# Where the gate products of the attention stand on TensorE, and where their bias rows come in

## The chip, the core and the metric

The kernel runs on one core of a Trainium2 chip, as one launch. The metric is the device time of that launch in microseconds; the time given for a kernel is the median of its runs. The engines are called PE (TensorE, products; PEld are its weight loads), DVE (VectorE), ACT (ScalarE), POOL (GpSimd) and SP (SyncE, which here only issues loads). Each engine works through its own queue in order. A load can be issued from the queues of SP, ACT and POOL.

## The reference, cut to what matters

One layer of an encoder trunk on 256 tokens of width 2048: windowed attention with 32 query heads and 8 key/value heads, and a squared-ReLU MLP of width 8192. Each of the two is preceded by a scale and shift and followed by a gated residual and a layer norm. Scale, shift and gate are one product of a single vector with a 2048 x 12288 matrix:

```python
c_act = jax.nn.silu(c)
mod = c_act @ mod_w[i] + mod_b[i]
sh_m, sc_m, g_m, sh_f, sc_f, g_f = jnp.split(mod, 6, axis=-1)
hmix = x * (1.0 + sc_m[:, None, :]) + sh_m[:, None, :]
y = windowed_gqa_sink(hmix, ...)             # ... @ w_o + b_o
x = layer_norm(DEEPNORM_ALPHA * x + (1.0 + g_m[:, None, :]) * y, ...)
hff = x * (1.0 + sc_f[:, None, :]) + sh_f[:, None, :]
y = sq_relu_mlp(hff, ...)                    # relu(hff @ w1 + b1) ** 2 @ w2 + b2
x = layer_norm(DEEPNORM_ALPHA * x + (1.0 + g_f[:, None, :]) * y, ...)
```

All numbers are float32. The change touches the two gates `g_m` and `g_f` and the output bias `b_o` of the attention.

## The kernel before

**Weights.** Every weight matrix is cut into blocks of 128 x 2048 floats, 1 MB each, which SP loads in one planned order into "raw" buffers (`Stream.loads`, the DMA of line 209): five buffers of the pool `raws`, and three more of `raws2` up to the middle of the attention. ACT casts each half of a block to a high part (`wh`, line 254) and DVE subtracts to get a low part (`wl`, line 225); five halves of each can be ahead of use. A product of activations with weights is then three matmuls, high by high, high by low and low by high: `mm3`, lines 501 to 503. PE does this work through the whole kernel.

**Modulation.** Between the weight blocks of that planned order stand the blocks of the modulation matrix. They need no split: `Mod.step` multiplies a block with the activated vector `cact`. For most blocks this is done on PE, as a quad of four small matmuls into one PSUM tile `pm`, one for each group of 32 columns of the array (`quad`, line 313). For the blocks listed in `dve` it is done on DVE, which keeps sums per partition in `part`: the first block by a multiply (line 351), the later ones by a multiply-add (line 353); at the end a matmul with a matrix of ones adds the partitions up. A modulation block is called a chunk here.

- `m_gm` is the gate of the attention, 16 chunks, loaded from `in_modgm`. Chunks 5, 9, 12 and 14 go to DVE, the others to PE. At its end a quad with `onesf` adds the sums of DVE, and a quad with `ones` adds the bias, which POOL loads into four small buffers `br` (line 336; tag "t2", four buffers) six chunks before the end.
- `m_gf` is the gate of the MLP, 16 chunks from `in_modgf`, all on DVE, in two `g4b` buffers, during MLP block 1. Its `step` passes through the same line 336 at chunk 10, and so loads four `br` tiles which nothing reads afterwards. At chunk 15, POOL loads the bias in four rows (line 331) and adds them to partition 0 of the sums (line 332).
- `m_mix` and `m_ff` are scale and shift of the two halves, from `in_modm` and `in_modf`; their biases are added elsewhere.

`gate` turns the finished sums into 128 equal rows by a product with ones (line 400). It is called for `m_gm` in step 12 of the attention and for `m_gf` in MLP block 2.

**The attention.** The loop `for n in range(21)` writes scores, softmax, transposes and values (`scores`, `normalise`, `probs_T`, `values`) of step n, and between them weight products: the last four blocks of the query/key/value product for n = 0 to 3, and from n = 5 on one column block of the output product, `project(j, c)`, with j = (n - 5) // 4. The outputs of j = 0 are added to the output bias `bo` (line 852), which `bias_all` spreads over all partitions by two loads from POOL's queue (line 178, 512 KB each) into two of the 20 buffers of the tag `g4`, at n = 0.

**Order.** The program is traced in the order of the code, and a planner then gives each engine its order: of the instructions that its own estimate of durations takes to be ready, the one traced first. So an instruction traced late may stand early on its engine. `Stream.pump` traces chunks ahead of the weight blocks that follow them, whenever a product is half or wholly done (`S.done`). `S.pin` holds the order of some instructions to that of the code, in the first stretch only. A tile takes the place of one that was released, and waits for that release.

**Buffers of the tag `g4b`.** The first call of `g4b` ends the pool `raws2` and puts six buffers of 128 x 1024 floats (`gen2`) in its place. Before the change the first call is at n = 5: four buffers for `ys`, the sums of the output product; at n = 12 two for the gate. After the attention they serve the sums of the MLP, its bias, and the sums and the gate of `m_gf`.

**MLP block 1.** `ff_hidden(1)` computes the hidden columns, four column groups of output products follow (`ff_out`), each evicted by line 1086. With each group, POOL loads two rows `gb` of the layer norm (line 1081, tag "t2" like `br`), and DVE applies them to the residual (lines 1090 and 1091).

Of the kernel before, what the change touches and what calls it, by code (L numbers as in the profile page):

```python
# [11 lines left out]
F32 = mybir.dt.float32  # L12
# [8 lines left out]
S = 256  # L21
# [19 lines left out]
NHIGH = 5  # L41
NLOW = 5
VECS = 2


@with_exitstack
def hybrid_kernel(ctx: ExitStack, tc: tile.TileContext, a, out: bass.AP):
# [17 lines left out]
    def g4b(dt=F32):  # L65
        if not more:
            early.close()
            more.append(ctx.enter_context(tc.tile_pool(name="gen2", bufs=2 * MORE)))
        return more[0].tile([128, 1024], dt, tag="g4b", name="g4b")
# [15 lines left out]
    make_identity(nc, ident)  # L85
    identr = cst.tile([128, 128], F32R, name="identr")
    nc.vector.tensor_copy(identr, ident)
    ones = cst.tile([1, 32], F32, name="ones")
    nc.vector.memset(ones, 1.0)
    onesr = cst.tile([128, 128], F32R, name="onesr")  # L90
    onesf = cst.tile([128, 128], F32, name="onesf")
    nc.vector.memset(onesf, 1.0)
# [81 lines left out]
    def bias_all(src, g4=g4):  # L174

        b = [g4(), g4()]
        for h in range(2):
            nc.gpsimd.dma_start(b[h], src[:, h * 1024:h * 1024 + 1024].partition_broadcast(128))
        return lambda c: b[c // 2][:, (c % 2) * 512:(c % 2) * 512 + 512]


    class Stream:
# [4 lines left out]
        def __init__(self):  # L187
            self.q, self.raw = [], []
            self.hs, self.ls, self.src = [], [], []
            self.free, self.home, self.used = [raws] * RAWS + [raws2] * MORE, [], 0  # L190
            self.of = []
            self.deep = True
            self.at = self.im = 0
            self.nh, self.nl = NHIGH, NLOW
            self.stop = 0
            self.pace = VECS
            self.pin = False
            self.side = {}

        def plan(self, src, use=None, kept=False):  # L200
# [91 lines left out]
    class Mod:  # L292
        def __init__(self, srcs, width, dve=(), bias=None):
            self.srcs, self.dve, self.bias = srcs, set(dve), bias
            self.pairs = width == 64
            self.w = 128 if self.pairs else width
            self.kc = 2048 // (4 * width)
            self.n = NK // self.kc
            self.i = self.planned = 0
            self.whole = len(self.dve) == NK  # L300
            self.first = True
            self.part = None

        def plan(self, n=1):
            for _ in range(n):
# [4 lines left out]
        def quad(self, lhsT, rhs, stop):  # L310
            w = self.w
            for j in range(4):
                i = nc.tensor.matmul(self.ps[32 * j:32 * j + 32, :w], lhsT[j] if type(lhsT) is list else lhsT,  # L313
                                     rhs[j], start=self.first, stop=stop)
                if j == 0:
                    S.pinned(i)
            self.first = False

        def step(self, raw):
            w, kc, i = self.w, self.kc, self.i  # L320
            if i == 0:
                self.ps = psm.tile([128, 512], F32, name="pm")
            r = raw.rearrange("p (k j n) -> p k j n", k=kc // 2 if self.pairs else kc, j=4)
            self.i += 1
            last = self.i == self.n
            per = 1024 // w
            if last and self.whole:
                for n in range(4):
                    b, p = sml.tile([128, 512], F32, name="mrow", bufs=2), self.part[n // 2]
                    p = p[0:1, n % 2 * 512:n % 2 * 512 + 512]  # L330
                    nc.gpsimd.dma_start(b[0:1], self.bias[:, n * 512:n * 512 + 512])
                    nc.gpsimd.tensor_add(p, p, b[0:1])
            elif i == self.n - 6 and self.bias is not None:
                self.br = [sml.tile([128, 512], F32, name="br", tag="t2", bufs=4) for _ in range(4)]
                for n, b in enumerate(self.br):
                    nc.gpsimd.dma_start(b[0:1], self.bias[:, n * 512:(n + 1) * 512])
            for k in range(kc):
                kt = i * kc + k
                if self.pairs:
                    if k % 2 == 0:  # L340
                        cols = [cact[:, kt + j // 2:kt + j // 2 + 1].to_broadcast([128, 32]) for j in range(4)]
                        self.quad(cols, [r[:, k // 2, j] for j in range(4)], last and k == kc - 2)
                elif i in self.dve:
                    e = min(4 * w, 1024)
                    new = self.part is None
                    if new:
                        self.part = [(g4b if self.whole else g4)() for _ in range(4 * w // e)]
                    for n, p in enumerate(self.part):
                        s = raw[:, k * 4 * w + n * e:k * 4 * w + n * e + e]
                        if new:  # L350
                            nc.vector.tensor_scalar(p[:, :e], s, cact[:, kt:kt + 1], None, op0=OP.mult)
                        else:
                            nc.vector.scalar_tensor_tensor(p[:, :e], s, cact[:, kt:kt + 1], p[:, :e],  # L353
                                                           op0=OP.mult, op1=OP.add)
                else:
                    stop = last and k == kc - 1 and not self.dve and self.bias is None
                    self.quad(cact[:, kt:kt + 1].to_broadcast([128, 32]), [r[:, k, j] for j in range(4)], stop)
            if last and not self.whole:
                if self.dve:
                    self.quad(onesf[:, :32], [self.part[j // per][:, (j % per) * w:(j % per) * w + w]  # L360
                                              for j in range(4)], self.bias is None)
                if self.bias is not None:
                    self.quad(ones, [b[0:1] for b in self.br], True)
                self.r = sml.tile([128, 512], F32, name="mrow", bufs=2)
                nc.scalar.copy(self.r[:, :w], self.ps[:, :w])

# [133 lines left out]
    def mm3(ps, xh, xl, wh, wl, start, stop):  # L500
        nc.tensor.matmul(ps, xh, wh, start=start, stop=False)  # L501
        nc.tensor.matmul(ps, xh, wl, start=False, stop=False)  # L502
        nc.tensor.matmul(ps, xl, wh, start=False, stop=stop)  # L503

    XK = [(0, 2), (2, 2), (4, 4), (8, 4), (12, 4)]

# [375 lines left out]
        return out  # L882

    todo = []
    for n in range(21):
        j, i = n // 4, n % 4
        if n < 16:
# [1 line left out]
        for f in todo:  # L889
            f()  # L890
        todo = []
        if n == 0:
            bo = bias_all(a["bo"])
        if n == 1:
            S.deep = False
        if n == 5:
# [1 line left out]
        if n + 2 < len(LATE):  # L898
            w = qkv(*LATE[n + 2])
        elif n < 5:  # L900
            w = iter((0, 1))
        else:
            if n == 5:
                ys = [g4b() for _ in range(4)]
            w = project((n - 5) // 4, (n - 5) % 4)
        S.vecs(SLOT_FILL.get(n, 0) if len(LATE) - 2 <= n < 5 else 0)
        mid = mids(n)
# [24 lines left out]
    def ff_columns(g):  # L932
# [4 lines left out]
        nc.vector.tensor_mul(b2[:, s], lnT[:, 1, s], scf[:, s])  # L937
        nc.vector.tensor_add(b2[:, s], b2[:, s], shf[:, s])

    ff_columns(0)  # L940
    S.stop = 0
    S.vecs(4)
# [272 lines left out]
```

## Time and profile before

| | us |
|---|---|
| median of 3 runs | 1149.16 |
| lowest and highest run | 1144.77, 1152.79 |
| the profiled execution | 1148.29 |
| its span, first to last instruction | 1146.5 |

Mean granted clock of TensorE in the profiled execution: 0.984 of full speed.

In the profile a row of the page's second part has one digit for each fortieth of the span, the busy share in tenths. In lists of instructions, "out<-in" are the program's tile names, and an idle time in brackets is that of the engine just before the instruction, with the instruction or load that ended it. A quad shows as eight matmuls, since a float32 matmul is two instructions. "L313" is line 313 of the kernel. Busy times of PE are modelled and overlap by some tenths of a microsecond.

The loads by source, with the median time from issue to landing in the profiled execution: blocks of `in_modgm` 6.2 us, of `in_modgf` 6.7, of `in_modf` 6.3, the two loads of the output bias 4.8, the `gb` rows 6.2.

### The profile page before, as it was taken

To read this page: it belongs to the slowest core of one execution; us is meant where nothing else is said; L and a number is where in the kernel's file an instruction comes from. 1 tells how busy PE (TensorE), PEld (TensorE's weight loads), DVE (VectorE), ACT (ScalarE), POOL (GpSimd) and SP (SyncE) were. 2 spreads that over 40 slices of the span, in tenths; PEclk is the share of its full clock that TensorE was granted. 3 is DMA by queue.
4 is the path that set the end of the run, shared out by engine and by line. 5 is a ranking of instruction groups with operands and counts; after the bars stand their busy time and mean duration, and the time that the engine had idled before them with its cause. 6 is when DMAs were issued, how large, how long until landed. Compare 5 with 4: busy or idle time off the path is not lost.

```text
span 1146.5 us, 15812 instructions
## 1 busy us (share of the span) xinstructions
PE 1096.7 (96%) x6258; PEld 882.3 (77%) x6258; DVE 810.3 (71%) x1122; ACT 546.9 (48%) x852; POOL 31.8 (3%) x52
## 2 busy tenths in 40 slices
PE   8889999699999999999999998998999999999994
PEld 6667666356776699988888886887888888888883
DVE  5697885757989978765578887756665656665656
ACT  5333554657775455653345542335444334444331
POOL 2000000000000000000000001300000000000001
PEclk9999999979999999999999998999999999999997
DMA  9999997626896798555677788764555555557511
GB/s 377 424 425 425 428 382 245 232 86 218 319 336 224 278 376 330 187 188 204 226 260 280 270 289 298 257 247 157 184 184 190 205 192 184 184 187 258 207 46 73
DMA packets 42946, 288.51 MB, mean 252 GB/s; under 512 B 5100, under 2 KB 5740, under 8 KB 9080
## 3 DMA queue, kind: packets, MB, share of 16 engines
q1 hardware_dynamic: 39824, 279.85, 65.3%
q0 software_dynamic: 2176, 6.32, 1.7%
q10 hardware_dynamic: 872, 1.34, 0.4%
q8 instruction: 49, 0.80, 0.3%
q14 instruction: 25, 0.20, 0.0%
HBM read 285.39 MB, written 2.10 MB: 251 GB/s over the span
## 4 chain that ended last, share of the span: by engine, by line
PE 80%; DMA 9%; DVE 6%; issue 2%; ACT 2%; POOL 0%; DVEq 0%; SPq 0%; ACTq 0%; POOLq 0%
PE pa L501 14%; PE pa L503 14%; PE pa L502 14%; PE pa L1045 13%; PE pa L1046 7%; PE pm L313 4%; DMA raw<-in_modm 3%; PE pa L1022 3%; PE pa L1021 3%; PE pa L1023 3%; DMA raw<-in_modgf 2%; DVE wl L225 2%; PE pa L792 1%; DMA raw<-in_wqkv 1%; PE pt L777 1%
## 5 line engine op out<-in xcount | busy, mean ns | idle before, releaser
L225 DVE TENSOR_TENSOR wl<-raw,wh 128x1024 fp32r<-128x1024 f32 x332 | 405.8, 1228 | 234.5 <-ACT wh L254 233.7
L254 ACT CAST wh<-raw 128x1024 fp32r<-128x1024 f32 x332 | 347.6, 1053 | 457.2 <-PE pa L503 241.5
L501 PE MATMUL pa<-wh,g 128*128 128x512 f32 x816 | 322.4, 396 | 11.3 <-DVE g4b L1086 5.2
L503 PE MATMUL pa<-wh,g 128*128 128x512 f32 x816 | 319.1, 393 | 1.3 <-DVE g L539 1.3
L502 PE MATMUL pa<-wl,g 128*128 128x512 f32 x816 | 319.7, 392 | 0.0
L1045 PE MATMUL pa<-g,wh 128*128 128x512 f32 x768 | 270.3, 397 | 2.9 <-DVE rl L994 2.9
L1046 PE MATMUL pa<-g,wl 128*128 128x256 f32 x768 | 215.5, 281 | 0.0
L501 PEld LDWEIGHTS pa<-wh,g 128*128 128x128 f32 x816 | 153.8, 189 | 52.3 <-DVE g4b L1086 5.9
L503 PEld LDWEIGHTS pa<-wh,g 128*128 128x128 f32 x816 | 153.6, 188 | 38.4 <-DVE g L539 3.4
L502 PEld LDWEIGHTS pa<-wl,g 128*128 128x128 f32 x816 | 154.0, 189 | 31.2 <-issue 1.0
L1045 PEld LDWEIGHTS pa<-g,wh 128*128 128x128 f32 x768 | 144.1, 188 | 38.2 <-DVE rl L994 3.6
L1046 PEld LDWEIGHTS pa<-g,wl 128*128 128x128 f32 x768 | 145.1, 189 | 0.2
L1022 PE MATMUL pa<-g,wh 128*128 128x256 f32 x256 | 72.7, 285 | 0.4 <-DVE g L965 0.4
L1021 PE MATMUL pa<-g,wh 128*128 128x256 f32 x256 | 72.5, 286 | 0.0
L1023 PE MATMUL pa<-g,wl 128*128 128x256 f32 x256 | 72.3, 283 | 0.0
L313 PE MATMUL pm<-raw,cact 128*32 128x256 f32 (+2 forms) x832 | 58.5, 381 | 14.2 <-DMA raw<-in_modgm 9.7
L353 DVE SCALAR_TENSOR_TENSOR g<-raw,cact,g 128x1024 f32<-128x1024 f32 x51 | 65.1, 1278 | 3.7 <-DMA raw<-in_modgm 3.2
L313 PEld LDWEIGHTS pm<-raw,cact 128*32 128x32 f32 x832 | 22.1, 109 | 36.2 <-DMA raw<-in_modgm 10.9
L1021 PEld LDWEIGHTS pa<-g,wh 128*128 128x128 f32 x256 | 48.8, 192 | 1.3 <-issue 0.8
L1022 PEld LDWEIGHTS pa<-g,wh 128*128 128x128 f32 x256 | 49.1, 192 | 0.9 <-DVE g L965 0.8
L1023 PEld LDWEIGHTS pa<-g,wl 128*128 128x128 f32 x256 | 49.1, 192 | 0.0
L353 DVE SCALAR_TENSOR_TENSOR g4b<-raw,cact,g4b 128x1024 f32<-128x1024 f32 x30 | 38.1, 1279 | 9.2 <-DMA raw<-in_modgf 6.8
(180 smaller groups left out, 854.2 us busy)
## 6 DMA issues: line engine op xcount, KB each, us to landing
raw<-in_w SPq DMA_DIRECT2D x64, 1024.0 KB, 4.9
raw<-in_w1b SPq DMA_DIRECT2D x48, 1024.0 KB, 5.0
raw<-in_modm SPq DMA_DIRECT2D x32, 1024.0 KB, 15.8
raw<-in_modf SPq DMA_DIRECT2D x32, 1024.0 KB, 6.3
raw<-in_wqkv SPq DMA_DIRECT2D x24, 1024.0 KB, 14.4
raw<-in_modgm SPq DMA_DIRECT2D x16, 1024.0 KB, 6.2
raw<-in_wo SPq DMA_DIRECT2D x16, 1024.0 KB, 6.5
raw<-in_w1a SPq DMA_DIRECT2D x16, 1024.0 KB, 6.8
```

The source lines that it names most:

```text
L225: self.pinned(nc.vector.tensor_sub(l, r, f32(self.hs[n])))
L254: self.pinned(nc.scalar.copy(h, s))
L313: i = nc.tensor.matmul(self.ps[32 * j:32 * j + 32, :w], lhsT[j] if type(lhsT) is list else lhsT, rhs[j], start=self.first, stop=stop)
L353: nc.vector.scalar_tensor_tensor(p[:, :e], s, cact[:, kt:kt + 1], p[:, :e], op0=OP.mult, op1=OP.add)
L501: nc.tensor.matmul(ps, xh, wh, start=start, stop=False)
L502: nc.tensor.matmul(ps, xh, wl, start=False, stop=False)
L503: nc.tensor.matmul(ps, xl, wh, start=False, stop=stop)
L1021: nc.tensor.matmul(o, wh(w, 128), hh, start=new, stop=False)
L1022: nc.tensor.matmul(o, wh(w, 128), hl, start=False, stop=False)
L1023: nc.tensor.matmul(o, wl(w, 128), hh, start=False, stop=end)
L1045: nc.tensor.matmul(ps, wh(k, 128), hb, start=k == 0, stop=False)
L1046: nc.tensor.matmul(ps[:, :256], wl(k, 128), hb[:, :256], start=False, stop=k == NK - 1)
```

## The change

1. In the attention loop (`S.behind`, set before the loop and cleared behind it), the first matmul of each quad gets an edge of order, without a wait, to the last matmul of the last `mm3` traced above it (`S.prev`). The planner may then not put the quad ahead of that matmul on PE.
2. The sums that DVE keeps for the two gates begin with the bias row. At chunk 4 of `m_gm` and chunk 0 of `m_gf` (`start`), POOL sets the two tiles of `part` to zero and two loads from ACT's queue put the bias into their partition 0. The first DVE chunk is then a multiply-add like the others. The `br` loads, the quad with `ones`, and POOL's loads and additions at the end of `m_gf` are gone.
3. `bias_all(a["bo"])` moves from n = 0 to n = 5 and takes its two buffers from `g4b`.

```diff
+ORDER_ONLY = mybir.DependencyInfo(mybir.DependencyClass.NoSync, mybir.DependencyReason.DATA)
...
-    ones = cst.tile([1, 32], F32, name="ones")
-    nc.vector.memset(ones, 1.0)
...
-            self.pin = False
+            self.pin = self.behind = False
+            self.prev = None
...
+            self.start = -1 if bias is None else max(min(dve) - 1, 0)
...
                 if j == 0:
                     S.pinned(i)
+                    if S.behind and S.prev is not None:
+                        tc.add_manual_dep(i.ins, S.prev.name, ORDER_ONLY, reason="behind")
...
-            if last and self.whole:
-                for n in range(4):
-                    b, p = sml.tile([128, 512], F32, name="mrow", bufs=2), self.part[n // 2]
-                    p = p[0:1, n % 2 * 512:n % 2 * 512 + 512]
-                    nc.gpsimd.dma_start(b[0:1], self.bias[:, n * 512:n * 512 + 512])
-                    nc.gpsimd.tensor_add(p, p, b[0:1])
-            elif i == self.n - 6 and self.bias is not None:
-                self.br = [sml.tile([128, 512], F32, name="br", tag="t2", bufs=4) for _ in range(4)]
-                for n, b in enumerate(self.br):
-                    nc.gpsimd.dma_start(b[0:1], self.bias[:, n * 512:(n + 1) * 512])
+            if i == self.start:
+
+                self.part = [(g4b if self.whole else g4)() for _ in range(2)]
+                for n, p in enumerate(self.part):
+                    nc.gpsimd.memset(p, 0.0)
+                    nc.scalar.dma_start(p[0:1], self.bias[:, n * 1024:n * 1024 + 1024])
...
-                    stop = last and k == kc - 1 and not self.dve and self.bias is None
+                    stop = last and k == kc - 1 and not self.dve
...
-                                              for j in range(4)], self.bias is None)
-                if self.bias is not None:
-                    self.quad(ones, [b[0:1] for b in self.br], True)
+                                              for j in range(4)], True)
...
-        nc.tensor.matmul(ps, xl, wh, start=False, stop=stop)
+        S.prev = nc.tensor.matmul(ps, xl, wh, start=False, stop=stop).ins
...
     todo = []
+    S.behind = True
     for n in range(21):
...
-        if n == 0:
-            bo = bias_all(a["bo"])
...
             if n == 5:
-                ys = [g4b() for _ in range(4)]
+                ys, bo = [g4b() for _ in range(4)], bias_all(a["bo"], g4b)
...
+    S.behind = False
     ff_columns(0)
```

More of the change, by code (lines that the diff above doesn't have):

```diff
@@ L346, in step @@
                     if new:
-                        self.part = [(g4b if self.whole else g4)() for _ in range(4 * w // e)]
+                        self.part = [g4() for _ in range(4 * w // e)]
                     for n, p in enumerate(self.part):
```

## The prediction

> **What bounds the kernel now.** I read the page first, then the list of who waited for whom on PE, then PE's idle stretches by windows, and last the timelines of the engines around them. The page:
>
> ```profile
> PE 1096.7 (96%) x6258; PEld 882.3 (77%) x6258; DVE 810.3 (71%) x1122; ACT 546.9 (48%) x852; POOL 31.8 (3%) x52
> ...
> PE   8889999699999999999999998998999999999994
> ...
> PEclk9999999979999999999999998999999999999997
> ```
>
> TensorE is the bound: it is busy 96% of the span, and each slice is 28.7 us. Behind the start its row dips in slice 7 (201 to 229 us, in the attention), 24 (688 to 717 us) and 27, and the granted clock dips in slices 8 and 24. So the room is in single stalls. The longest waits of PE over the whole run (total us, times, longest us):
>
> ```profile
> PE pm L313 <- DMA raw<-in_modgm: 9.7, 2, 9.0
> PE pa L501 <- DVE g4b L1086: 5.2, 1, 5.2
> ...
> PE pa L1045 <- DVE rl L994: 2.9, 2, 2.6
> ```
>
> The first is a gate chunk of the attention (a step of `m_gm`) that waits for its load, the second a weight product of MLP block 1 that waits for an eviction. What each costs, by windows (us; busy PE, PEld, DVE, ACT, POOL; granted clock; DMA share; GB/s):
>
> ```profile
> 221.30:230.30 9.00, 0.00 (x0) 0.00 (x0) 5.68 (x7) 1.70 (x4) 0.00 (x0) 0.70 0.70 274
> 230.30:236.00 5.70, 5.69 (x20) 1.05 (x21) 0.04 (x1) 1.07 (x2) 0.00 (x0) 0.50 0.84 282
> 236.00:243.00 7.00, 7.00 (x39) 5.05 (x39) 1.46 (x4) 2.75 (x5) 0.00 (x0) 0.57 0.18 73
> 243.00:255.00 12.00, 12.00 (x58) 7.87 (x58) 9.35 (x21) 9.50 (x30) 0.00 (x0) 1.00 0.00 1
> 698.50:703.80 5.30, 0.06 (x2) 0.01 (x1) 5.30 (x8) 0.00 (x0) 0.54 (x1) 0.91 0.95 322
> 703.80:709.70 5.90, 5.90 (x14) 4.64 (x15) 5.90 (x7) 1.04 (x1) 0.54 (x1) 0.51 0.96 310
> 776.30:779.10 2.80, 0.19 (x3) 0.02 (x1) 1.60 (x3) 1.42 (x2) 0.00 (x0) 1.00 0.78 234
> 779.10:785.00 5.90, 5.90 (x33) 5.16 (x34) 5.33 (x10) 3.58 (x7) 0.00 (x0) 1.00 0.16 67
> ```
>
> A long stall is paid twice: behind the 9.0 us one the clock is 0.50 for 5.7 us and 0.57 for 7.0 us, which loses 5.7 x 0.50 + 7.0 x 0.43 = 5.9 us; behind the 5.3 us one it is 0.51 for 5.9 us, 2.9 us lost. The 2.6 us wait at 776 is followed by full clock. So the first stall is worth at most 9.0 + 5.9 = 14.9 us and the second 5.2 + 2.9 = 8.1 us.
>
> [...]
>
> **The change, part by part. (A) The order of gate chunks.** PE in order of time (start, us, what, count, idle before and its releaser):
>
> ```profile
> 206.46 0.39 PE L503 MATMUL pa<-wh,g 128*128 128x512 f32 x1
> 206.78 1.06 PE L313 MATMUL pm<-raw,cact 128*32 128x512 f32 x8
> ...
> 218.09 1.06 PE L313 MATMUL pm<-raw,cact 128*32 128x512 f32 x6 [0.73 <-DMA raw<-in_modgm]
> ...
> 230.31 1.93 PE L313 MATMUL pm<-raw,cact 128*32 128x512 f32 x8 [9.01 <-DMA raw<-in_modgm]
> 232.01 1.93 PE L313 MATMUL pm<-g,onesf 128*32 128x512 f32 x8
> 233.88 1.91 PE L313 MATMUL pm<-br,ones 1*32 1x512 f32 x2
> 235.72 1.25 PE L706 MATMUL pt<-identr,g 128*128 128x128 f32 x8
> ...
> 245.54 0.50 PE L501 MATMUL pa<-wh,g 128*128 128x512 f32 x1
> ```
>
> Following `pump` by hand, the code traces chunk 13 (at 218.09) behind the first half of `project(0, 0)`, whose first product is the row at 245.54, and chunk 15 with the closing `onesf` and `br` products (230.31 to 238) behind the first half of `project(0, 1)`, later still. The planner had moved them 27 us and more ahead of those products, taking their loads as landed. Most other chunks run right behind the product traced above them already, as at 206.78. The new edge puts these two groups back, so PE, done with the transposes at 221.3, meets the head transposes L706 next, not a chunk whose load is on its way. Only the first quarter of each quad carries the edge; the others add to the same bank and follow.
>
> How much of the 14.9 us comes? What PE then runs needs the vector engine and its loads:
>
> ```profile
> 219.09 1.22 DVE L225 TENSOR_TENSOR wl<-raw,wh 128x1024 fp32r<-128x1024 f32 x1
> ...
> 227.86 2.48 DVE L353 SCALAR_TENSOR_TENSOR g<-raw,cact,g 128x1024 f32<-128x1024 f32 x2 [3.22 <-DMA raw<-in_modgm]
> 241.12 0.43 DVE L741 TENSOR_TENSOR pa<-pa,msk 128x256 f32<-128x256 f32 x1 [10.78 <-PE pa L739]
> ```
>
> The mask add of the next scores stands at 241.12, behind the two multiplies of chunk 14, which wait for their load until 227.86 and end at 230.34. No edge holds those. So the softmax chain can move up by 241.12 - 230.34 = 10.8 us. Meanwhile PE has transposes, score products and `project(0, 0)`, whose last low half (the L225 at 219.09) is ready. Upper end 14.9, chain 10.8; I take 9, because bo now loads there too (below). Lower end 0: another wait takes the place at once. Held in order, chunks 13 and 15 keep their raw buffers longer, and loads on SP's queue behind those buffers start later; the DMA share of 0.00 at 243 to 255 shows that no load was outstanding there and that there is room to catch up, so I take nothing for it (rival 4 prices it).
>
> **(B) The output bias in `g4b` buffers.** Gone from `g4`, it frees 2 of 20 buffers. On POOL:
>
> ```profile
> 1.91 0.96 POOL L159 MEMSET g<- 128x1024 f32 x1
> ...
> 190.70 0.53 POOL L178 DMA_DIRECT2D g<-in_bo  x1 [13.00 <-PE pt L777]
> ...
> 681.83 0.51 POOL L336 DMA_DIRECT2D br<-in_modgfb  x1 [5.35 <-ACT g L998]
> ...
> 687.82 0.48 POOL L336 DMA_DIRECT2D br<-in_modgfb  x1 [3.23 <-DMA br<-in_modgfb]
> 688.38 0.57 POOL L1081 DMA_DIRECT2D gb<-in_lnrow  x1
> ```
>
> The two loads of bo leave 177 to 191 us and need the early raw buffers, the last of which is read by the L225 at 219.09. So they start near 220, 1 MB beside the loads of chunks 14 and 15. At the 274 GB/s of that window it is 3.8 us of traffic, of which the idle 0.30 of 9 us, 2.7 us, takes most; chunk 14 may land 1 to 2 us later. That is what I take off the 10.8 us. The first use, behind `project(0, 0)`, comes no earlier than about 231 us, so bo itself isn't late.
>
> [...] If all of the 3.8 us fell on chunk 14, A would be 7 us and not 9; no run here shows it yet.
>
> **(C) Bias rows first.** Removed: eight `br` products of `m_gm` (two groups, the first of them above), in a quad that takes 1.06 us at full clock by the row at 218.09: 1 us less on PE. For `m_gf` the four `br` loads were issued too (681.83 to 687.82) and never read; they take the four "t2" buffers and POOL's queue ahead of the `gb` row at 688.38. The second stall hangs on it:
>
> ```profile
> 694.84 0.69 DVE L1090 SCALAR_TENSOR_TENSOR g<-g,gb 128x512 f32<-128x512 f32 x1 [5.08 <-DMA gb<-in_lnrow]
> ...
> 703.05 1.27 DVE L1086 TENSOR_TENSOR g4b<-g4b,pa 128x512 f32<-128x512 f32 x2
> ```
>
> DVE waits 5.08 us for `gb`, so the eviction L1086 comes at 703.05, though PE had finished by 698.5. Without `br`, `gb` takes the buffers that came free at 681.83: 6.5 us earlier, more than the wait. PE's idle time falls to about one eviction, 0.6 us, too short to cost the clock: 8.1 - 0.6 = 7.5. The planner may place L1090 earlier with it and leave a wait of a us; I take 7, ends 0 and 8.1.
>
> Added: each first multiply becomes multiply-add, four memsets, four loads on ACT's queue.
>
> ```profile
> L353 DVE SCALAR_TENSOR_TENSOR g4b<-raw,cact,g4b x30: 1275/1278/1287, 575.2 to 744.8; 128x1024 f32<-128x1024 f32 x30
> ...
> L351 DVE TENSOR_SCALAR g4b<-raw,cact x2: 741/742/744, 563.9 to 565.7; 128x1024 f32<-128x1024 f32 x2
> ```
>
> ```profile
> L1132 ACTq DMA_DIRECT2D out<-g x4: 338/352/383, 1132.9 to 1141.5; - x4
> ```
>
> ```profile
> mrow<-in_modgfb POOLq DMA_DIRECT2D x4, 2.0 KB, 4.6
> ```
>
> DVE: 4 x (1.278 - 0.742) = 2.1 us over the run, hidden at 71% load. POOL: 4 x 0.96 us, idle anyway. ACT: 4 x 0.35 = 1.4 us at 48% load; behind each waiting issue ACT's casts stand until POOL's memset is done, 1 us. For `m_gf` the sum starts in the very step that needs it, where its second buffer comes free (about 564): memset 0.96 us, issue 0.35, landing 4.6 as the small rows above, some 6 us before L353 may run. What covers it is the lead of up to five split weight buffers and DVE's idle time. I take 0; ends 0 and the second stall's own price, 8.1 us. The four POOL additions into the finished `m_gf` sums go as well; no PE wait names them: 0.
>
> **The sum.** -9 - 7 - 1 = -17 us on the profiled execution of 1148.29 us (span 1146.5, 1.8 us around it; 0.87 under the median 1149.16): 1131.3 us, and I give 1131. All gains full: -14.9 - 8.1 - 1 = -24, 1124.
>
> **The rivals.** (1) Only the second stall goes: PE leaves the chunk and meets scores that wait for DVE, still behind chunk 14. For it speaks the 3.22 us wait at 227.86, against it the ready product work: 1148.3 - 8 = 1140. (2) Only the first goes: L1090 is planned earlier by as much as `gb` is and still holds L1086; 1148.3 - 10 = 1138. (3) No change: new short waits of the planner's new order eat all; 1148. (4) Slower: held raw buffers. Loads leave SP's queue in order, so a chunk kept behind a late product holds every load behind it, weights too. Each load that then comes late at PE costs what chunk 15 did, a landing of about 6 us and about 3 of clock, 9 us; two such cancel the 17 us, four make 1167. It decides from the third late load on. Against it stands the idle DMA after 243.
>
> **How the numbers follow.** Forecast 0.52, rivals 0.18, 0.12, 0.10 and 0.08. A measurement of this kernel can tell about 1% from no change (1137.7 and 1160.7). The forecast's own range, 1122 to 1137, counts as faster; of rivals 1 and 2, both near the bound, a third of 0.30 does: 0.52 + 0.10 = 0.62. Slower takes rival 4, cut to the part beyond 1160: 0.06. The same: 0.32. The range reaches from full gains with a few us for a roomier planner, 1120, to no change, 1148.
>
> **What would show it.** Right for A: no wait of PE on in_modgm near 220, clock 1.0 from 221 to 255, chunk 15's products behind those of the projects. For C: no `br` row, `gb` two loads in a row near 665 (17 us shifts included), no wait of DVE for it over 2 us, PE's wait before the second column group of block 1 under 1 us. For the ends: a DVE wait for the bias row at the first `m_gf` step, with PE idle behind it, or PE waiting for in_modf or `wh` between 240 and 390. The forecast is wrong if PE is idle in the attention for as long as before, whoever is named.

## The result, and the profile after

| | before | after |
|---|---|---|
| median, us (runs) | 1149.87 (4) | 1136.85 (4) |
| lowest and highest run, us | 1144.77, 1152.79 | 1135.22, 1137.36 |
| the profiled execution's span, us | 1146.5 | 1135.0 |
| mean granted clock in it | 0.984 | 0.990 |

The ratio after to before is 0.9889, its 95% interval 0.9852 to 0.9926. Six more runs of it beside eleven of before, on another chip, gave 0.9901, 0.9878 to 0.9924 (e11 below). The change makes the kernel about 1% faster, some 11 to 13 us. One of the six runs of e7 below took 2763.18 us; its ratio is that of the other five.

The page of the kernel after: busy times, PE's busy tenths in 40 slices of 28.4 us, and its granted clock.

```profile
PE 1088.9 (96%) x6250; PEld 880.2 (78%) x6250; DVE 811.0 (71%) x1121; ACT 546.7 (48%) x852; POOL 21.7 (2%) x40
...
PE   8889999799999999999999999999999999999994
...
PEclk9999999999999999999999999999999999999997
```

The dips of slices 24 and 27 are gone, and so are those of the clock. Slice 7 (199 to 227 us), in the attention, still has one: 7, where 6 stood. The longest waits of PE (us in total, times, longest) say what stands there now:

```profile
PE pm L314 <- DMA raw<-in_modm: 4.4, 6, 1.4
...
PE pt L703 <- ACT g L776: 3.2, 1, 3.2
PE pa L1042 <- DVE rl L991: 2.9, 2, 2.6
...
PE pa L498 <- DVE g4b L1083: 2.4, 1, 2.4
```

The wait for `in_modgm`, 9.7 us before, is not in the list any more. In its place PE waits 3.2 us for a copy of ACT that belongs to the softmax's transposes. The wait for the eviction (L1083, formerly L1086) has fallen from 5.2 to 2.4 us. The windows around both (us; busy PE, PEld, DVE, ACT, POOL; granted clock; DMA share; GB/s):

```profile
221.50:224.80 3.30, 0.12 (x2) 0.04 (x1) 3.06 (x6) 3.30 (x12) 0.00 (x0) 1.00 0.98 345
224.80:232.00 7.20, 5.88 (x33) 5.37 (x33) 3.12 (x5) 4.88 (x10) 0.00 (x0) 0.53 0.66 279
...
691.00:693.50 2.50, 0.14 (x2) 0.05 (x1) 2.50 (x5) 0.00 (x0) 0.54 (x1) 1.00 0.97 360
693.50:700.00 6.50, 6.50 (x29) 5.38 (x30) 6.50 (x8) 2.12 (x2) 0.00 (x0) 1.00 0.94 290
```

The idle time in the attention is short, 3.2 us, but the clock behind it is 0.53 for 7.2 us. The shorter one in block 1, 2.4 us, is followed by full clock.

**Where the time went.** To split the gain by place, take the start of the same product in each trace and subtract its start in the trace of before. A negative number is time gained up to that point. The points are the 51st call of `mm3` (78.9 us before, early in the kernel), the first product of `project(0, 0)` (245.5), the first product of the MLP (397.9), the first of the second column group of MLP block 1 (711.4) and the last call of `mm3` (1129.4). The kernels e1 to e12 are told of below.

| us against before | 51st | project(0, 0) | MLP | block 1, group 2 | last | attention alone |
|---|---|---|---|---|---|---|
| after | +2.8 | -10.1 | -7.4 | -13.1 | -11.7 | -10.2 |
| e11, after again | +0.7 | -10.3 | -7.7 | -9.8 | -8.5 | -8.4 |
| e7, after with the tile `ones` | +2.1 | -11.1 | -8.5 | -13.4 | -10.5 | -10.6 |
| e1, after without the edge | +3.1 | -8.2 | -4.0 | -7.1 | -4.2 | -7.1 |
| e4, before with bo moved | +0.2 | -22.0 | -17.5 | -16.7 | -16.8 | -17.7 |
| e2, e4 with the edge | +0.2 | -21.9 | -17.7 | -18.0 | -16.6 | -17.9 |
| e8, before with bo late in `g4` | +1.1 | -20.6 | -15.9 | -16.6 | -14.8 | -17.0 |
| e5, e4 with bias rows first in `m_gf` | +1.6 | -20.5 | -16.2 | -17.9 | -16.5 | -17.8 |
| e6, after with the gate's sums late | +1.9 | -19.6 | -16.9 | -19.5 | -19.6 | -18.8 |
| e9, e6 without the edge | +3.3 | -17.9 | -13.4 | -16.7 | -15.3 | -16.7 |
| e10, e6, gate chunks of block 1 moved | +3.0 | -19.1 | -15.9 | -23.8 | -20.1 | -18.9 |
| e12, the same, moved further | +1.7 | -20.5 | -17.7 | -24.6 | -20.5 | -19.4 |
| e3, before without the dead loads | +0.9 | -1.5 | -1.3 | -4.2 | -2.8 | -2.2 |

The last column is MLP minus 51st. Apart from e3 it falls into two groups: 7 to 11 us, and 17 to 19. The kernel after is in the first. A single trace can't be read to better than about 2 us here: after and e11 are the same program and differ by 2.1 us at the 51st product, but not at `project(0, 0)` or the MLP. So the last column overstates the gain of after by about that much, and -7.4 and -7.7, the column MLP, are the safer figures for it. The experiments were about what puts a kernel into the second.

### The profile page after: what moved, and what is told of

The parts are those of the page before. It is cut to its first block, busy times and chain, and to the rows that moved or that the text cites. A ratio compares the mean times of both kernels' runs of the same rounds, so it can differ in the third digit from the quotient of the medians.

```text
span 1135.0 us, 15765 instructions
## 1 busy us (share of the span) xinstructions
PE 1088.9 (96%) x6250; PEld 880.2 (78%) x6250; DVE 811.0 (71%) x1121; ACT 546.7 (48%) x852; POOL 21.7 (2%) x40
## 4 chain that ended last, share of the span: by engine, by line
PE 82%; DMA 7%; DVE 6%; ACT 3%; issue 1%; DVEq 0%; ACTq 0%; SPq 0%
PE pa L1042 15%; PE pa L498 14%; PE pa L500 14%; PE pa L499 14%; PE pa L1043 8%; DMA raw<-in_modm 4%; PE pm L314 3%; PE pa L1019 3%; PE pa L1018 3%; PE pa L1020 3%; DVE wl L225 2%; PE pa L789 1%; DMA raw<-in_wqkv 1%; PE pt L774 1%; ACT wh L254 1%
## 5 line engine op out<-in xcount | busy, mean ns | idle before, releaser
L500 PE MATMUL pa<-wh,g 128*128 128x512 f32 x816 | 318.9, 392 | 1.7 <-DVE g L536 1.7
L500 PEld LDWEIGHTS pa<-wh,g 128*128 128x128 f32 x816 | 153.2, 188 | 38.5 <-DVE g L536 3.6
L352 DVE SCALAR_TENSOR_TENSOR g<-raw,cact,g 128x1024 f32<-128x1024 f32 x53 | 68.0, 1283 | 0.4
L314 PE MATMUL pm<-raw,cact 128*32 128x256 f32 (+2 forms) x832 | 54.8, 379 | 5.4 <-DMA raw<-in_modm 4.4
L352 DVE SCALAR_TENSOR_TENSOR g4b<-raw,cact,g4b 128x1024 f32<-128x1024 f32 x32 | 40.6, 1282 | 7.5 <-DMA raw<-in_modgf 5.2
```

What stands on the lines that cost most here:

```text
L500: S.prev = nc.tensor.matmul(ps, xl, wh, start=False, stop=stop).ins
```

## The experiments

The ratios are to the runs of the kernel before on the same chip, with 95% intervals.

### Which part carries the gain: e1 to e4

e1 is the kernel after with the edge never switched on:

```diff
-    S.behind = True
```

> The changed kernel without the edge of order (the bias rows and the output bias as changed). Theory: the edge alone removes the stall on the gate chunk in the attention. Then PE waits for in_modgm again, about 9 us, with 12 us of halved clock behind it, and the run is about 10 us longer than the changed kernel, 1145 to 1149 us, while the stall in MLP block 1 stays short (under 3 us) and no DVE wait for gb comes back. Rival: the output bias in other buffers gave the planner its room, and the stall went with that; then PE has no wait over 3 us for in_modgm and the time stays at 1135 to 1139 us.

Measured: 1140.46 us, ratio 0.9942 (0.9921 to 0.9963). Its profiled execution, the one in the table, is the slowest of its seven runs, 1144.21 us. The time lies between the two ranges, and the theory's mechanism isn't there: PE never waits for `in_modgm`, though no edge holds chunk 15. It stands just ahead of `project(0, 0)` (PE of e1):

```profile
235.54 1.07 PE L314 MATMUL pm<-raw,cact 128*32 128x512 f32 x8
236.42 1.02 PE L314 MATMUL pm<-g,onesf 128*32 128x512 f32 x2
237.37 0.50 PE L498 MATMUL pa<-wh,g 128*128 128x512 f32 x1
```

e4 is the kernel before with the output bias moved, and nothing else:

```diff
-        if n == 0:
-            bo = bias_all(a["bo"])
...
-                ys = [g4b() for _ in range(4)]
+                ys, bo = [g4b() for _ in range(4)], bias_all(a["bo"], g4b)
```

> The kernel before with the output bias in g4b buffers and nothing else. Theory: no effect beyond 3 us; the gate chunk still stalls PE for 8 to 12 us in the attention and gb for 5 us in block 1; 1146 to 1152 us. Rival: two g4 buffers more let the planner order the attention otherwise and the stall on in_modgm shrinks below 4 us; then 1137 to 1143 us.

Measured: 1132.08 us, ratio 0.9869 (0.9843 to 0.9895). The theory fell. The rival had the direction, PE's wait for `in_modgm` is gone, but the time is 5 us under its range.

e2 is e4 with the edge of the change:

```diff
+                    if S.behind and S.prev is not None:
+                        tc.add_manual_dep(i.ins, S.prev.name, ORDER_ONLY, reason="behind")
...
-        nc.tensor.matmul(ps, xl, wh, start=False, stop=stop)
+        S.prev = nc.tensor.matmul(ps, xl, wh, start=False, stop=stop).ins
...
+    S.behind = True
     for n in range(21):
...
+    S.behind = False
```

> The kernel before with the edge and with the output bias in g4b buffers, the bias rows as before. Theory: the attention gains what the changed kernel gains there, about 10 us, and MLP block 1 keeps its stall: a DVE wait for gb of about 5 us, a PE wait of about 5 us before the second column group and halved clock behind it; 1139 to 1142 us. Rival: the second stall hung on the phase that block 1 reaches and not on the br loads; then it is gone or under 3 us here too, and the time is 1134 to 1137 us.

Measured: 1132.69 us, ratio 0.9870 (0.9848 to 0.9893). This is below both ranges. The second stall is there as the theory said (PE waits 5.3 us for the eviction), but the attention alone gains 17.9 us, not 10.

e3 is the kernel before without the four loads of `br` that `m_gf` never reads:

```diff
-            elif i == self.n - 6 and self.bias is not None:
+            elif i == self.n - 6 and self.bias is not None and not self.whole:
```

> The kernel before, without the four br loads of m_gf that nothing reads. Theory: they alone make the second stall, by the four buffers and POOL's queue; PE's wait before the second column group of block 1 falls from 5.2 us to under 3, the clock stays whole, and the run is 5 to 8 us shorter than before, 1142 to 1144 us; the attention keeps its 9 us wait. Rival: the bias rows first (no POOL additions, sums opened early) do it; then the wait stays at 5 us and the time at 1147 to 1151 us.

Measured: 1147.28 us, ratio 1.0000 (0.9982 to 1.0017). The time is the rival's. In the trace the loads do count: DVE's wait for `gb` falls to 0.5 us and PE's for the eviction from 5.2 to 3.4. PE's wait for `in_modgm` stays, 8.6 us.

What follows: moving bo is enough by itself, and by the medians and the traces it brings more than the whole change (the intervals of the two ratios overlap). The edge adds nothing to it (e2 and e4, 1132.69 and 1132.08). The dead loads alone are worth nothing that can be measured, though by the table about 3 us come between the MLP's start and group 2 (-1.3 to -4.2). The kernel before with the edge alone, and the kernel after with bo back at n = 0, were not tried.

**Why bo, whose loads seemed only a cost?** The answer is on ACT, 25 us ahead of the stall. The scores of step 1 are done early in every kernel, as PE's rows of before and after show (start, us, count):

```profile
184.23 0.28 PE L738 MATMUL pa<-g,g 128*128 128x256 f32 x1
```

```profile
187.14 0.28 PE L735 MATMUL pa<-g,g 128*128 128x256 f32 x1
```

The first exponential of that step comes much later. POOL's rows of before, then ACT's rows of before up to that exponential (L752; in brackets the idle time and what ended it):

```profile
177.12 0.58 POOL L178 DMA_DIRECT2D g<-in_bo  x1 [168.47 <-PE pt L706]
```

```profile
198.69 0.21 ACT L754 ACTIVATE es<-es 128x4 f32<-128x4 f32 x1 [4.75 <-DVE es L748]
204.17 1.05 ACT L254 CAST wh<-raw 128x1024 fp32r<-128x1024 f32 x1 [5.27 <-PE pa L503]
205.57 1.05 ACT L254 CAST wh<-raw 128x1024 fp32r<-128x1024 f32 x1 [0.35 <-PE pa L503]
206.53 0.46 ACT L752 ACTIVATE g<-pa,nm 128x256 f32<-128x256 f32 x1
```

POOL and ACT of e4:

```profile
200.78 1.11 POOL L178 DMA_DIRECT2D g4b<-in_bo  x2 [192.13 <-DVE es L748]
```

```profile
191.37 0.21 ACT L754 ACTIVATE es<-es 128x4 f32<-128x4 f32 x1 [1.99 <-DVE es L748]
191.97 0.47 ACT L752 ACTIVATE g<-pa,nm 128x256 f32<-128x256 f32 x1 [0.40 <-DVE g L670]
```

The scores stand at 184 us in both, the exponential at 206.53 and at 191.97. In between ACT is nearly idle in the kernel before, busy for 3.2 of the 14.9 us from 191.6 to 206.5. The exponential writes a tile of the tag `g4`; of the 20 buffers, bo takes two at 177 and 191 us, just ahead of that tile in the order of the code. The tile then has to wait until the last query/key/value products release theirs (the profile names such a release in the kernel after, below). It stands 14.6 us later than in e4, the next exponentials 8.7 us (211.39 and 202.66). So PE runs out of other work at 221 us and meets chunk 15. In e4 no edge holds chunk 15, and the planner puts it far behind `project(0, 0)`, without a wait (PE, e4):

```profile
223.56 0.50 PE L501 MATMUL pa<-wh,g 128*128 128x512 f32 x1 [0.37 <-ACT g L752]
```

```profile
245.62 1.06 PE L313 MATMUL pm<-raw,cact 128*32 128x512 f32 x8
```

### What takes the buffers back in the changed kernel: e6 and e8

The kernel after moves bo and yet has the late exponential. POOL and ACT of after:

```profile
179.78 0.95 POOL L334 MEMSET g<- 128x1024 f32 x1 [173.20 <-PE pt L703]
193.14 0.96 POOL L334 MEMSET g<- 128x1024 f32 x1 [12.41 <-PE pt L774]
```

```profile
204.95 0.21 ACT L751 ACTIVATE es<-es 128x4 f32<-128x4 f32 x1 [8.09 <-DVE es L745]
207.26 1.05 ACT L254 CAST wh<-raw 128x1024 fp32r<-128x1024 f32 x1 [2.11 <-PE pa L500]
209.85 0.48 ACT L749 ACTIVATE g<-pa,nm 128x256 f32<-128x256 f32 x1 [1.54 <-PE pa L500]
```

The two zeroed tiles are the sums of `m_gm`, which now open at chunk 4. They take two `g4` buffers at about the times at which bo's loads took them, 179.78 and 193.14 for 177.12 and 190.70. And here the profile names what the exponential waits for: the product L500, the one that releases the buffer. Chunk 4 is traced ahead of the scores of step 1, chunk 5 behind them. So e6 opens the sums one chunk later:

```diff
-            self.start = -1 if bias is None else max(min(dve) - 1, 0)
+            self.start = -1 if bias is None else min(dve)
```

> The changed kernel, with the sums of m_gm opened at chunk 5, the first that DVE takes, and not at chunk 4. Theory (two g4 buffers held early): chunk 5 is traced behind the scores of step 1, so their exponentials get a buffer first and start near 193 us; the attention becomes 6 to 10 us shorter than in the changed kernel; 1126 to 1131 us. Rival (bias first itself costs: memset on POOL, load on ACT's queue, multiply-adds): no change, 1134 to 1139 us, exponentials of step 1 still behind 205 us.

Measured: 1129.46 us, ratio 0.9824 (0.9800 to 0.9848). POOL and ACT of e6:

```profile
196.09 0.95 POOL L334 MEMSET g<- 128x1024 f32 x1 [189.53 <-DVE g L669]
197.64 0.95 POOL L334 MEMSET g<- 128x1024 f32 x1 [0.60 <-PE pa L736]
206.67 1.25 POOL L177 DMA_DIRECT2D g4b<-in_bo  x2 [8.07 <-DVE wl L225]
```

```profile
194.24 0.48 ACT L749 ACTIVATE g<-pa,nm 128x256 f32<-128x256 f32 x1 [2.39 <-DVE g L667]
```

The theory held. The exponential stands at 194.24, 15.6 us earlier than in the kernel after. It now waits for DVE's L667, as that of e4 does for L670 of its kernel (the same statement), and no longer for a product. The kernel is 7 us faster: this one index had taken away over a third of what the change could bring.

e8 asks whether the pool matters or only the place. It is the kernel before with bo traced at n = 5, still in two `g4` buffers:

```diff
-        if n == 0:
-            bo = bias_all(a["bo"])
...
-                ys = [g4b() for _ in range(4)]
+                ys, bo = [g4b() for _ in range(4)], bias_all(a["bo"])
```

> The kernel before with the output bias loaded at n = 5, still into two g4 buffers. Theory: when the buffers are taken decides, not from which pool; the exponentials of step 1 start near 192 us, and the time is that of bo in g4b buffers, 1130 to 1136 us. Rival: the pool decides, since the planner loads ahead whenever a g4 buffer is free; then the exponentials stay near 206 us and the time at 1144 to 1151 us.

Measured: 1130.55 us, ratio 0.9835 (0.9810 to 0.9861). It is as good as e4, and the exponential is early again, though bo still takes two `g4` buffers, between 215 and 235 us (ACT of e8):

```profile
193.35 0.48 ACT L752 ACTIVATE g<-pa,nm 128x256 f32<-128x256 f32 x1 [0.40 <-DVE g L670]
```

So what decides is when the buffers are taken, not from which pool they come.

### The smaller terms: e5, e7, e9 and e11

e5 is e4 with the bias rows first in `m_gf` alone; `m_gm` stays as before, and there is no edge:

```diff
-            if last and self.whole:
-                for n in range(4):
...
-            elif i == self.n - 6 and self.bias is not None:
+            if i == 0 and self.whole:
+                self.part = [g4b() for _ in range(2)]
+                for n, p in enumerate(self.part):
+                    nc.gpsimd.memset(p, 0.0)
+                    nc.scalar.dma_start(p[0:1], self.bias[:, n * 1024:n * 1024 + 1024])
+            elif i == self.n - 6 and self.bias is not None and not self.whole:
```

> The kernel before with the output bias in g4b buffers and, for m_gf alone, the bias rows first (no br loads, no POOL additions); m_gm keeps its bias products at the end; no edge. Theory now: the attention stall comes from two g4 buffers held at 180 to 206 us, by bo before and by the sums of m_gm in the changed kernel; without either the first exponentials of step 1 start near 192 us as with bo moved alone (206.5 before, 209.8 changed), and the second stall shrinks by 3 to 6 us; 1125 to 1129 us. Rival: the two gains do not add, because block 1 reaches another phase; then it stays at 1130 to 1134 us.

Measured: 1131.25 us, ratio 0.9835 (0.9812 to 0.9858). The time is in the rival's range. Against e4 (0.9869) the intervals overlap; PE's wait for the eviction in block 1 is 3.6 us where e4 has 6.1.

e7 is the kernel after with the tile `ones` left in place, unused, which shifts the addresses of what is behind it:

```diff
+    ones = cst.tile([1, 32], F32, name="ones")
+    nc.vector.memset(ones, 1.0)
```

> The changed kernel with the small tile ones kept, which nothing reads: every later tile then lies 128 bytes higher, as before. Theory: the load rate of the first 110 us, 419 GB/s in the changed kernel against 425 before, hangs on where the raw buffers lie; it returns to 425 and the products at 80 us come 2 to 3 us earlier; 1132 to 1135 us. Rival: the rate differs from run to run; it stays at 419 or moves with no tie to the tile, 1135 to 1138 us.

Measured: 1137.94 us, ratio 0.9888 (0.9862 to 0.9915): no change of the time that can be measured. But half of the theory held: the load rate does hang on the tile. From 50 to 100 us it is 426 GB/s in e7 and 425 in before, e4, e5 and e8, which keep the tile too, and 419 GB/s in after, e6, e9, e10 and e11, which don't. The 1.4% between 425 and 419 doesn't bring the later products forward by the 2 to 3 us that the theory asked for: the 51st product is at +2.1 us here, and +2.8 and +0.7 in after and e11.

e11 is the kernel after once more, without an edit.

> The changed kernel itself, once more. Theory (the later start, the 51st weight product at 81.6 us and not 78.9, and the slower pairs of MLP block 2, 2.83 us and not 2.77, belong to the program): the 51st product at 81.6 within 0.4 us and the pairs at 2.83 again, 1136.9 within 2 us. Rival (they differ from one execution to the next): the product elsewhere between 79 and 82 us, or the pairs at 2.77, and a time within the same 1135 to 1139.

Measured: 1139.98 us, ratio 0.9901 (0.9878 to 0.9924), 1 us above what either side expected. The slower products of block 2 came again (last section), the later start did not. The 51st product stands at 79.6 us, not 81.6. The 2.8 us that the kernel after seemed to lose at its start belong to the one execution, in which the clock was 0.97 from 50 to 100 us; here it is 1.00. The gain in block 1 is 2.1 us (-7.7 to -9.8), where the first trace had 5.7: PE's wait there is 3.3 us and not 2.4, and the mean clock from 680 to 730 us is 0.93, where in the first trace the wait is followed by full clock.

e9 is e6 without the edge:

```diff
-    S.behind = True
```

> The kernel whose gate sums open at chunk 5 (1129.46 us), without the order edge. Theory (the edge only matters while the two g4 buffers are held; with them free the first exponential of step 1 stands near 194 us and PE has product work, so the order of chunks 13 and 15 decides nothing): within 1.5 us of 1129.5, first MLP product within 1 us of 381.0. Rival (the 3.6 us between the changed kernel with and without its edge, 1136.85 and 1140.46, are the edge's own and are independent of the buffers): 1133, first MLP product near 384.5 and a wait of PE on in_modgm.

Measured: 1133.39 us, ratio 0.9858 (0.9835 to 0.9880), slower than e6 by 4 us in the medians and by 0.3% in the ratios, whose intervals just overlap. The theory that the edge does nothing once the buffers are free fell: the time and the start of the MLP (384.5 us) are the rival's. But the rival's mechanism isn't there either: PE never waits for `in_modgm`. By the table its attention alone gains 2.1 us less than that of e6 (16.7 and 18.8); 1.4 us of the rest lie ahead of the 51st product and 1.4 in MLP block 2. Between e1 and the traces of after, e11 and e7 the edge's share is 1.3 to 3.5 us (7.1 against 8.4 to 10.6), between e4 and e2 nothing (17.7 and 17.9). So the edge is worth 0 to 3.5 us in the attention (0 to 4.5 by the column MLP), and 2 us of that are within the spread of two traces of one program. Whether the order that the planner finds around it decides, and which, stays open.

### What is left of the second stall: e10 and e12

With `br` gone, DVE no longer waits for `gb`. POOL and DVE of after, ahead of the eviction (L1083):

```profile
666.46 0.54 POOL L1078 DMA_DIRECT2D gb<-in_lnrow  x1 [130.63 <-ACT g L995]
667.98 0.54 POOL L1078 DMA_DIRECT2D gb<-in_lnrow  x1 [0.98 <-DVE g L996]
```

```profile
680.55 1.22 DVE L225 TENSOR_TENSOR wl<-raw,wh 128x1024 fp32r<-128x1024 f32 x1
685.11 1.29 DVE L352 SCALAR_TENSOR_TENSOR g4b<-raw,cact,g4b 128x1024 f32<-128x1024 f32 x1 [3.34 <-DMA raw<-in_modgf]
...
692.72 1.28 DVE L1083 TENSOR_TENSOR g4b<-g4b,pa 128x512 f32<-128x512 f32 x2
```

A gate chunk of the MLP, waiting for its load, has taken the place of `gb`. e10 is e6 with no chunk of `m_gf` in the first column group of block 1; its two go to groups two and three:

```diff
-                if blk == 1 and kg % 2:
+                if blk == 1 and c and (kg % 2 or c < 3 and kg == 2):
                     m_gf.plan()
```

> The kernel whose gate sums open at chunk 5 (1129.46 us), with no m_gf chunk planned in the first column group of MLP block 1 (its two chunks go to the second and third group, three there instead of two). Theory (what is left of the second stall is DVE's wait for a late in_modgf load, 3.52 us at 677.1, ahead of the eviction in line 1083): that DVE wait ahead of the first group's eviction is under 0.5 us, PE's wait for g4b L1083 falls from 3.8 to under 1 us, the slower clock behind it (1.2 us) goes too, 1125. Rival (loads are what is short there, DMA share 0.87 from 660 to 700 us: the wait moves to a weight block or to a later group's chunk): a PE wait of 2 us or more in the next group, 1128.5 to 1131.

Measured: 1128.34 us, ratio 0.9804 (0.9784 to 0.9825). In the first group the theory holds: up to group 2 block 1 gains 7.9 us (-15.9 to -23.8), where e6 gains 2.6. Then the rival holds: PE waits in the next group, where the loads are denser (DMA share 0.94 from 690 to 720 us, 0.82 in e6; PE, then the windows of e10):

```profile
706.83 0.50 PE L498 MATMUL pa<-wh,g 128*128 128x512 f32 x1 [2.06 <-DVE g4b L1083]
```

```profile
660.00:690.00 30.00, 29.91 (x132) 24.45 (x131) 26.57 (x31) 11.98 (x14) 3.27 (x7) 1.00 0.94 342
690.00:720.00 30.00, 27.94 (x124) 22.82 (x123) 26.97 (x29) 11.01 (x11) 0.00 (x0) 1.00 0.94 342
```

e12 moves the chunks on, to groups three and four:

```diff
-                if blk == 1 and c and (kg % 2 or c < 3 and kg == 2):
+                if blk == 1 and c and (kg % 2 or c > 1 and kg == 2):
```

> The kernel with no m_gf chunk in the first column group of MLP block 1 (1128.34 us), but with the two moved chunks in the third and fourth group instead of the second and third, where the DMA share is 0.66 from 720 to 750 us and not 0.94. Theory (the 2.1 us wait for g4b L1083 at 706.8 came from the chunk that was put into the second group): the first group's gain stays (the second column group of block 1 begins at 687.6), the wait at 706.8 falls under 1 us, and the block is 2 to 3 us shorter: 1126. Rival (DVE and the loads are full from 660 to 720 us whichever chunk stands there, and the wait moves one group further): a wait of 2 us or more of PE for g4b in a later group, 1128 to 1130.

Measured: 1128.30 us, ratio 0.9821 (0.9798 to 0.9844). The wait of 2.1 us is gone, and PE waits for the eviction three times, 3.2 us in all and none over 1.2:

```profile
PE pa L498 <- DVE g4b L1083: 3.2, 3, 1.2
```

The time is the rival's, not the 1126 of the theory, but the rival's long wait didn't come. e6, e10 and e12 can't be told apart by their times: all three are about 1.8 to 2.0% under before and some 8 us under the change. With DVE busy 26 to 27 of 30 us and the DMA share at 0.94 in e10, the stage seems to have little left to give by moving chunks about; that was argued from these shares, not shown.

## Why the prediction was right, and where not

The time, 1131, was 6 us too low, and faster by over 1%, the likeliest case, came true by a small margin (1136.85 against a bound of 1137.7; e11 alone, at 0.9901, would have missed the 1%). The time lies at the very end of the forecast's own range, 1122 to 1137. The steps fared differently.

**The first stall: the size nearly right, by luck; the cause only half.** The forecast was 9 us for the edge and 1 for the `br` products; the attention alone gave 10.2, and 8.4 in e11 (7.4 and 7.7 by the column MLP). The step that failed is the one which gave all 9 us to the edge, because the chunk was taken to be the whole cause. Without the edge (e1) PE doesn't wait for `in_modgm` either, and 7.1 us of the gain stay. What the prediction didn't see is that PE had no other work for want of an exponential 14.6 us late, which waited for a buffer: with that one early and the chunk free to go anywhere, bo alone gives 17.7 us (e4). That the sum still came near 10 us is chance: the edge was given too much, bo's buffers nothing, and the gate's early sums took back 8 (both below).

The other half of its reading isn't refuted. In after the exponential is as late as in before (209.85 and 206.53), but chunk 15 stands behind the stall, and PE waits for 3.2 us at a time in place of 9.0; in e1, where the chunk stands behind it too, for 1.9. So these rows suggest that the chunk's place made the stall longer. What moves the chunk back in e1, where no edge holds it, is not shown. The missing `br` loads of `m_gf` alone don't do it, since e3 keeps the 8.6 us.

**The output bias: not costed.** The prediction said in one sentence that bo's move frees 2 of 20 `g4` buffers, and then counted only its loads, as a cost of up to 2 us. The freed buffers are the largest term of all. What was missing was the way back from the first PE instruction behind the stall through what fed it, to ACT's rows at 191 to 206 us, where ACT is idle and the scores have long been there. The loads, on the other hand, cost nothing visible. They leave at 209.88 in after and at 200.78 in e4, not near 220, and neither PE in the whole run nor, in after, DVE around them waits for `in_modgm`. The case in which all 3.8 us of their traffic fall on chunk 14 and the edge brings 7 us and not 9 was an estimate of the prediction's; no run shows such a price.

**The early opening of the gate's sums: costed at nothing, worth 8.** Under "added" the prediction counted memsets, small loads and multiply-adds, each with its duration, and asked what hides them. It didn't ask which buffers the two tiles hold and from when. By the attention's own times, 10.2 us in after and 18.8 in e6, opening them one chunk early costs 8.6 us (9.5 by the column MLP).

**The second stall: mechanism right, size below the forecast.** `gb` is issued at 666.46, no load of `br` stands ahead of it, and DVE doesn't wait for it for 2 us anywhere. The step gave 5.7 us for the predicted 7 in one execution and 2.1 in the other (PE's wait 2.4 and 3.3 us). The end "0 to 8.1" held. The term was too large because DVE's next wait, a late chunk of `m_gf`, was not priced; when it is taken away too, the first group gives 7.9 us (e10) and 6.9 (e12), around the 7.5 worked out. The prediction also took what would be left of PE's wait, 0.6 us, as too short to cost the clock; the 3.3 us of e11 were not (mean clock 0.93 from 680 to 730 us).

**The first chunk of `m_gf`: right.** The memsets run at 383.59 and 534.88, both ahead of the 564 that the prediction expected for the second. DVE does wait for the bias load, but PE works through it at full clock (DVE, then PE's window of after):

```profile
560.26 1.29 DVE L352 SCALAR_TENSOR_TENSOR g4b<-raw,cact,g4b 128x1024 f32<-128x1024 f32 x1 [2.16 <-DMA g4b<-in_modgfb]
```

```profile
555.00:575.00 20.00, 20.00 (x90) 16.57 (x89) 14.30 (x14) 7.58 (x8) 0.00 (x0) 1.00 0.69 246
```

**The signs that were named.** Right: no wait on `in_modgm`, chunk 15 behind both projects (at 258.42), no `br` row. Wrong: the clock is not 1.0 from 221 to 255 (0.53 from 224.8 to 232), and PE's wait in block 1 is 2.4 us, not under 1. Together they said that a part of each gain was missing, and of the rivals none had the cause: the held buffers of rival 4 were the right kind of thing in the wrong pool, `raw` for `g4`, and held by the kernel before as well.

**Not foreseen:** 1.4 us are lost again in the hidden columns of MLP block 2 (below).

## What to carry to other kernels

A wait of the bounding engine names the last link of a chain. Before pricing the wait's removal, follow the next useful instruction back until an engine is idle with its inputs ready; a buffer held elsewhere shows as just that. When an edit opens or moves a tile of a rotating pool, price the buffers it takes, with the time from which it holds them, and not only its instructions: two tiles taken 16 and 4.5 us early cost more here than every instruction added. And when one late load is taken out of a queue of late loads, the next one is the price that is left: here DVE's 3.34 us for a chunk of `m_gf`, behind the 5.08 for `gb`.

## What the runs showed of the hardware that was not expected

**The same wait, with and without a slower clock.** A wait of 2.61 us at the start of block 2's hidden columns is followed by full clock in some executions and by a slow stretch in others. PE of after, then of e10 (start, us, idle before):

```profile
765.92 0.50 PE L1042 MATMUL pa<-g,wh 128*128 128x512 f32 x1 [2.61 <-DVE rl L991]
773.73 0.50 PE L1042 MATMUL pa<-g,wh 128*128 128x512 f32 x1 [0.26 <-DVE rl L991]
```

```profile
757.54 0.80 PE L1042 MATMUL pa<-g,wh 128*128 128x512 f32 x1 [2.61 <-DVE rl L991]
766.76 0.51 PE L1042 MATMUL pa<-g,wh 128*128 128x512 f32 x1 [0.26 <-DVE rl L991]
```

The same work takes 7.81 us in one and 9.22 in the other. From 765.9 to 773.7 us the granted clock of after is 1.00; in e10 it is 0.75 from 757.5 to 764. e8 is like e10: its 128x512 products behind the wait take 0.63 us; in before, e4, e5 and e9 they take 0.40 over 2.8 us and more, as in after. So a wait of 2.61 us can be followed by a slower clock, though in before, as the prediction's rows show, it isn't. The wait of 3.18 us in the attention of after is followed by 7.2 us at 0.53. What decides between the two outcomes of the same wait is not shown.

**Products 2% slower by program.** The 128x512 products of block 2's hidden columns have a mean of 392 ns in before and 399 ns in after, at a granted clock of 1.00 in both (line, form and count from 785 to 845 us; busy us, mean ns):

```profile
L1045 PE MATMUL pa<-g,wh 128*128 128x512 f32 x167 | 58.1, 392 | 0.3 <-DVE rl L994 0.3
```

```profile
L1042 PE MATMUL pa<-g,wh 128*128 128x512 f32 x171 | 60.5, 399 | 0.0
```

Over some 200 such products that is the 1.4 us. It is 399 ns again in e11, so it goes with the program and not with the execution; e6 and e10 have 391. In block 1 (520 to 660 us) and block 3 (900 to 1020 us) the mean is 399 ns in before and after alike: it is the faster case that is special. It doesn't go with the tile `ones`, which before keeps and e6 and e10 don't. What in the program sets it stays open: the number and the form of the instructions are the same.
